# Two-layer decoder trunk: mixed operands of the output projection on VectorE, later block loads, one inverse root chain

## The chip, the cores and the metric

The kernel runs on one core of a Trainium2 chip. The metric is the device time of one execution in microseconds (us), the median of several. Below, PE is TensorE, DVE is VectorE, ACT is ScalarE, POOL is GpSimd, and SP is the sync engine, which here only issues DMAs. Each engine works through its own instructions in order, and an instruction that waits on a semaphore holds up everything behind it on its engine.

## The reference

Two residual layers on x of 1024 tokens by 1024 features, in float32. Cut to what matters:

```python
# layer 1: gated short convolution, width 2048
h = rms_norm(x, conv_norm)
b, c, u, z = split(h @ w_in, 4)          # w_in: 1024 x 8192
y = b * conv3(c * u) * silu(z)           # causal, depthwise, 3 taps
x1 = x + y @ w_out                       # w_out: 2048 x 1024
# layer 2: dilated attention, 3 groups of 16 heads of 64
h = rms_norm(x1, attn_norm)
qkv, z = h @ w_in2                       # q and k are RMS-normed per head
o = softmax-weighted merge of 3 dilated window attentions with a T5 bias
out = x1 + (o * silu(z)) @ w_out2
```

The RMS norm divides each token by a root mean square, so it is a factor per token, and the kernel applies it after the projection, as one over the root.

## The kernel before

**Matrix products.** Every float32 operand is split into a rounded part and a rest (a "block" is four 128x512 tiles with both parts), and a product of 128x512 outputs over 512 inputs is 12 matmuls (`product`, L303: L307 rounded by rounded, L309 rounded weight by rest, L310 the weight's rest). The split of a weight is `split_w`: a copy on ACT (L160), then a subtraction on DVE (L161).

**Seven products for eight.** Most of the projections go in pairs of weight columns through a Strassen scheme: seven products instead of eight. The loop `strassen` (L322) runs over pairs; within a pair the products come in the order 1, 2, 4 (of the pair before), 6, 5, 3 (of the pair before), 7. "Slot `at`" is the place of a product in that order, 0 to 6, and `between(n, at)` is called behind product `at` of pair n for the extra work that is spread over the pairs. `prepare` (L267) yields the weights of the next pair one slot at a time; four of its seven weights are sums and differences that POOL makes (tile `sr`, L281), each then split by L160 and L161. The moving operands are mixed likewise: blocks T[1] to T[4] are differences of the quarters of x (or y), B the plain ones.

Products 1, 6, 7 and 4 (4 runs in the next pair) accumulate in one PSUM tile `x`. ACT copies it out after product 1 (`m1`) and after product 6 (`u2`), both by L315; the product that comes next on that tile, 6 or 7, overwrites nothing before this copy has read it. So product 7 waits for the copy `u2`, and product 6 for the copy `m1`.

**The stages.** Layer 1's input projection is pairs 0 to 28 (NI = 29), each width block e of 128 channels taking two pairs, c and u with pr = 0, z and b with pr = 1. The results go through the gate (ACT's L371, POOL's L372, L584, L599), the taps (L378 to L380), DVE's L602 and L612, and `close` (L386), and are written to DRAM `ydc` (L387). The output projection of layer 1, by `out_pair` (L499), is pairs NI to NI+3 for one half of the width; its mixed operands are four differences of quarters of y, in DRAM `ymd`. The other half comes in plain products, `chunk` and `row` (L683, L688): `row(hf, dt)` loads the partial sum from DRAM `x1d` (L692), adds the product (L693), writes x1 back, and makes from it the operands of layer 2 (blocks e, f, d, the block `xb`, and tiles V1 and V3), and x1's square summed into `sqacc` on POOL (L721). Then come the pairs of layer 2's projection, numbered from 0 again.

**What the change touches.**
- `y_mix(i)` (L491), called at slot 0 of the four pairs with pr = 1 and e from 6 to 9: SP loads four tiles of `ydc` (L494), POOL subtracts four times (L496) and writes each difference to `ymd` (L497, issued by POOL).
- `moves` (L623): at which slot which block of the output projection is loaded by SP and split by ACT (L480) and DVE (L481).
- `stats` (L93): four matmuls of one column sum `sqacc` over partitions, L97 scales, and `rsqrt` (L59) runs a chain of ten small DVE steps (L63, then three times L65, L66, L67). Before, it runs for token half 0 at slot 3 of layer 2's pair 0 and for half 1 at slot 1 of pair 1. `spread` (L100) turns a column of the result into a row for all partitions by four PE transposes (L105); `rtok` goes to R1 (by ACT, L107), which the pairs with v and z use, and `ms2` through DVE (L111, L112) to a small tile for the norm of q and k.
- `third`, `fourth`, `lower` (L905 to L920): blocks T[3], T[4] and B[1, 1] of layer 2, made at the slots of the table `rest`. `fourth` and `lower` load x1 from DRAM (L677); `fourth` starts with the DVE step L914.

**What sets the order.** PE, and in places the other engines, run in program order. Elsewhere the Tile scheduler merges the engines' work by its own estimate, so the place of a DVE or POOL instruction can differ from the place in the code. Tiles named `f` come from a pool of 12 buffers, so a load into one waits for the release of the tile twelve before.

## Time and profile before

| | before |
|---|---|
| median of 3 runs | 1931.04 us (1928.29 to 1932.02) |
| the profiled execution, its own time | 1936.98 us |
| its span from first to last instruction | 1934.9 us |
| mean granted TensorE clock | 0.991 |
| busy PE | 1883.5 us (97%) |
| busy PE weight loads | 1541.6 us (80%) |
| busy DVE | 1518.0 us (78%) |
| busy ACT | 884.8 us (46%) |
| busy POOL | 978.2 us (51%) |
| HBM read and written | 194.62 MB and 76.03 MB |

All times of the trace are counted from the span's start. In a table of windows, each engine has its busy time and, in brackets, the number of instructions; PEclk is the clock that TensorE was granted, as a share of full speed. In a timeline, the first two columns are start and duration, and square brackets hold the time for which the engine stood idle ahead of the instruction and what ended it. In a list of waits, the columns are the total, the number of times and the longest.

The stages along the span: the start up to about 270 us, pairs with `y_mix` from 271 to about 420 us, the rest of layer 1's input projection to about 640 us, the output projection to about 818 us, layer 2's projection to about 1606 us, attention and the last projection from there to the end.

### The profile page before, as it was taken

How to read it: one execution, taken by the hardware profiler on the slowest of the kernel's cores; microseconds unless marked ns; L12 is line 12 of the kernel's file. 1: busy time of each engine (PE TensorE's matmuls, PEld its weight loads, DVE VectorE, ACT ScalarE, POOL GpSimd, SP SyncE). 2: the span in 40 equal slices, each digit the busy share in tenths (PEclk: the TensorE clock that was granted, in tenths of full speed). 3: DMA queues.
4: the chain of work that ended last, by engine and by line, in shares of the span. 5: the costliest groups of instructions: out<-in, count | busy, mean ns of one | idle time of the engine just before them, and what ended most of it. 6: DMA issues, size and time to landing. Idle time of an engine off the chain costs nothing. (4 is left out here: it accounts for less than half of the span.)

```text
span 1934.9 us, 30577 instructions
## 1 busy us (share of the span) xinstructions
PE 1883.5 (97%) x10814; PEld 1541.6 (80%) x10814; DVE 1518.0 (78%) x2789; ACT 884.8 (46%) x2039; POOL 978.2 (51%) x910
## 2 busy tenths in 40 slices
PE   8999999999999999989999999999999998989999
PEld 6888887778888788868888888888888886777877
DVE  7966778877665855678888788868888886988886
ACT  6533333333433534443344344434444437878880
POOL 1376677776666453525445544564454552433340
PEclk9999999999999999999999999999999999899999
DMA  6222234332323765323324332433232336897742
GB/s 220 78 80 89 88 104 151 126 129 90 92 73 92 264 226 207 131 82 109 110 87 136 104 112 85 136 104 112 85 131 88 131 126 242 258 298 229 228 143 88
DMA packets 121514, 264.29 MB, mean 137 GB/s; under 512 B 19134, under 2 KB 24478, under 8 KB 121360
## 3 DMA queue, kind: packets, MB, share of 16 engines
q1 hardware_dynamic: 94432, 178.99, 28.6%
q0 software_dynamic: 26928, 83.34, 12.9%
q8 instruction: 85, 1.39, 0.3%
q14 instruction: 69, 0.57, 0.1%
HBM read 194.62 MB, written 76.03 MB: 140 GB/s over the span
## 5 line engine op out<-in xcount | busy, mean ns | idle before, releaser
L161 DVE TENSOR_TENSOR ws<-sr,ws 128x512 fp32r<-128x512 f32 x288 | 270.0, 943 | 95.8 <-ACT ws L160 93.9
L160 ACT ACTIVATE ws<-sr 128x512 fp32r<-128x512 f32 x288 | 180.6, 630 | 353.8 <-PE pp L310 254.0
L281 POOL TENSOR_TENSOR sr<-wr 128x512 f32<-128x512 f32 x144 | 209.4, 1454 | 245.9 <-DMA wr<-in_conv_w_in 96.5
L161 DVE TENSOR_TENSOR ws<-wr,ws 128x512 fp32r<-128x512 f32 x248 | 267.5, 1080 | 78.6 <-ACT ws L160 78.0
L160 ACT ACTIVATE ws<-wr 128x512 fp32r<-128x512 f32 x248 | 155.7, 629 | 290.6 <-PE pp L310 243.5
L319 DVE TENSOR_TENSOR f<-pp,f 128x512 f32<-128x512 f32 x216 | 147.6, 683 | 70.2 <-PE pp L310 63.1
L1058 ACT ACTIVATE xs<-xs,nl 128x256 f32<-128x256 f32 (+2 forms) x384 | 160.8, 428 | 0.0
L315 ACT ACTIVATE f<-pp 128x512 f32<-128x512 f32 x240 | 139.4, 581 | 4.1 <-PE pp L310 4.0
L281 POOL TENSOR_TENSOR sr<-wr,sr 128x512 f32<-128x512 f32 x72 | 95.5, 1327 | 70.1 <-issue 59.1
L307 PE MATMUL pp<-blka,ws 128*128 128x512 f32 x328 | 127.8, 390 | 0.7 <-ACT f L315 0.7
L307 PE MATMUL pp<-blkb,ws 128*128 128x512 f32 x328 | 128.0, 390 | 0.0
L310 PE MATMUL pp<-blkb,ws 128*128 128x512 f32 x328 | 127.6, 389 | 0.0
L309 PE MATMUL pp<-blka,ws 128*128 128x512 f32 x328 | 127.6, 389 | 0.0
L310 PE MATMUL pp<-blka,ws 128*128 128x512 f32 x328 | 127.6, 389 | 0.0
L309 PE MATMUL pp<-blkb,ws 128*128 128x512 f32 x328 | 127.6, 389 | 0.0
L307 PE MATMUL pp<-blkg,ws 128*128 128x512 f32 x320 | 125.2, 391 | 2.1 <-ACT f L315 2.1
L310 PE MATMUL pp<-blkg,ws 128*128 128x512 f32 x320 | 125.2, 391 | 0.0
L309 PE MATMUL pp<-blkg,ws 128*128 128x512 f32 x320 | 125.2, 391 | 0.0
L307 PE MATMUL pp<-blke,ws 128*128 128x512 f32 x288 | 113.9, 396 | 10.0 <-ACT f L315 10.0
L1052 DVE CUSTOM_DVE_ANT_0 xs<-ps,bt 128x256 f32<-128x256 f32 (+2 forms) x384 | 102.7, 326 | 20.4 <-PE pt L1065 11.8
L307 PE MATMUL pp<-blkf,ws 128*128 128x512 f32 x296 | 117.6, 397 | 0.5 <-ACT f L315 0.5
L309 PE MATMUL pp<-blkd,ws 128*128 128x512 f32 x296 | 115.6, 391 | 0.0
(329 smaller groups left out, 5055.9 us busy)
## 6 DMA issues: line engine op xcount, KB each, us to landing
wr<-in_conv_w_in SPq DMA_DIRECT2D x128, 256.0 KB, 3.2
wr<-in_wqk SPq DMA_DIRECT2D x96, 256.0 KB, 3.2
qkd<-blkc POOLq DMA_DIRECT2D x48, 512.0 KB, 4.0
qk<-qkd SPq DMA_DIRECT2D x48, 512.0 KB, 5.1
f<-in_x SPq DMA_DIRECT2D x48, 256.0 KB, 4.5
f<-ydc SPq DMA_DIRECT2D x48, 256.0 KB, 5.6
wr<-in_wv SPq DMA_DIRECT2D x48, 256.0 KB, 3.1
vd<-blkc POOLq DMA_DIRECT2D x96, 128.0 KB, 2.8
```

Of the source, the lines that this page charges most:

```text
L160: nc.scalar.activation(t[:, 0], src, AF.Copy)
L161: nc.vector.tensor_tensor(t[:, 1], src, t[:, 0].bitcast(F32), op=OP.subtract)
L281: nc.gpsimd.tensor_tensor(t, x, y, op=op)
L307: nc.tensor.matmul(ps, w[:, 0, ws], b[:, k, 0], start=new and k == 0, stop=False, skip_group_check=skip)
L309: nc.tensor.matmul(ps, w[:, 0, ws], b[:, k, 1], start=False, stop=False, skip_group_check=skip)
L310: nc.tensor.matmul(ps, w[:, 1, ws], b[:, k, 0], start=False, stop=end and k == 3, skip_group_check=skip)
L315: nc.scalar.activation(t, ps, AF.Copy)
L319: nc.vector.tensor_tensor(m, ps, m, op=OP.add)
L1052: nc.vector.tensor_tensor_reduce(out=x, in0=flat[s][:, cols], in1=u["bt"][s][:, bs], op0=OP.add, op1=OP.min, scale=-1.0, scalar=3e38, accu ...
L1058: nc.scalar.activation(x, x, AF.Exp, bias=nm, scale=-1.0, accum_out=L)
```

## The change

1. `y_mix` is cut into single steps. Instead of four differences at once in each of four pairs, one difference is made in each of the pairs 9 to 24, called at slot 2: SP loads the one or two tiles that are still missing, DVE subtracts (L509 of the changed file), POOL issues the write (L510).
2. Four of the loads of mixed blocks in the output projection come later: T[2] into block g from slot 3 to slot 4 of pair NI, T[1] into c from slot 4 to 6, T[3] into e from slot 5 to 8 (pair NI has ten slots), T[4] into f from slot 7 of pair NI to slot 3 of pair NI+1.
3. `stats` handles all eight columns at once, at slot 4 of layer 2's pair 0, and the four spreads run at slots 2 to 5 of pair 1, `ms2` first, `rtok` second.
4. `fourth(0)` to `fourth(2)` and `lower(0)` to `lower(2)` move from the slots of layer 2's first two pairs into the loop over rows, behind `row(0, 7)` and ahead of `row(1, 3)` and `row(1, 7)`. `fourth(3)` and `lower(3)` stay in pair 0, at slots 5 and 6.

```diff
-    def stats(hf, pool, tmp):
-        h4 = slice(4 * hf, 4 * hf + 4)
+    def stats(pool, tmp):
         ps = pool.tile([P, HALF], F32, name="st", tag="st")
-        mean_square(tmp, sqacc, ps, 4, lambda t, j: t[:, hf * HALF + j * P:hf * HALF + (j + 1) * P])
-        nc.vector.tensor_scalar(ms2[:, h4], ps[:, :4], 1.0 / D, EPS, op0=OP.mult, op1=OP.add)
-        rsqrt(tmp, ms2[:, h4], 4, "rt", rtok[:, h4])
+        mean_square(tmp, sqacc, ps, 8, lambda t, j: t[:, j * P:(j + 1) * P])
+        nc.vector.tensor_scalar(ms2, ps[:, :8], 1.0 / D, EPS, op0=OP.mult, op1=OP.add)
+        rsqrt(tmp, ms2, 8, "rt", rtok)
...
-            def y_mix(i):
-                a11, a12, a22, a21 = (ftile() for _ in range(4))
-                for t, hf, e in ((a11, 0, i), (a12, 1, i), (a22, 1, i + 4), (a21, 0, i + 4)):
+            ym = {}
+
+            def y_mix(i, n):
+
+                def load(hf, e):
+                    t = ftile()
                     nc.sync.dma_start(t, ydc[hf, e])
-                for n, (t, x, y) in enumerate(((a12, a12, a11), (a22, a22, a12), (a11, a22, a11), (a21, a21, a22))):
-                    nc.gpsimd.tensor_tensor(t, x, y, op=OP.subtract)
-                    nc.gpsimd.dma_start(ymd[n + 1, i], t)
+                    return t
+
+                if n == 0:
+                    ym["a"], t = load(0, i), load(1, i)
+                    y = ym["a"]
+                elif n == 1:
+                    t, y = load(1, i + 4), ym.pop("v")
+                elif n == 2:
+                    t, y = ym.pop("a"), ym["v"]
+                else:
+                    t, y = load(0, i + 4), ym.pop("v")
+                x, y = (y, t) if n == 2 else (t, y)
+                nc.vector.tensor_tensor(t, x, y, op=OP.subtract)
+                nc.gpsimd.dma_start(ymd[n + 1, i], t)
+                if n < 2:
+                    ym["v"] = t
...
-                     (NI, 3): lambda: y_mixed(2, "g"), (NI, 4): lambda: y_mixed(1, "c"),
-                     (NI, 5): lambda: y_mixed(3, "e"), (NI, 7): lambda: y_mixed(4, "f"),
+                     (NI, 4): lambda: y_mixed(2, "g"), (NI, 6): lambda: y_mixed(1, "c"),
+                     (NI, 8): lambda: y_mixed(3, "e"), (NI + 1, 3): lambda: y_mixed(4, "f"),
...
-                if pr and not at and 6 <= e < 10:
-                    y_mix(e - 6)
+                if at == 2 and 0 <= n - 9 < 16:
+                    y_mix((n - 9) // 4, (n - 9) % 4)
...
+                    elif hf == 0:
+                        for j in range(3):
+                            fourth(j)
+                        for j in range(3):
+                            lower(j)
...
-                if (n, at) in ((0, 3), (1, 1)):
-                    stats(n, cst, sm)
-                elif (n, at) in ((0, 6), (1, 5)):
-                    spread(n, rtok, cst)
-                elif (n, at) in ((1, 0), (1, 6)):
-                    spread(at // 6, ms2, cst)
+                if (n, at) == (0, 4):
+                    stats(cst, sm)
+                elif n == 1 and 2 <= at < 6:
+                    spread(at % 2, ms2 if at < 4 else rtok, cst)
...
-            rest = {0: [(third, 0), (third, 1)], 1: [(third, 2)], 2: [(third, 3)], 3: [(fourth, 0), (fourth, 1)],
-                    4: [(fourth, 2)], 5: [(fourth, 3), (lower, 0)], 6: [(lower, 1), (lower, 2)], 7: [(lower, 3)]}
+            rest = {0: [(third, 0), (third, 1)], 1: [(third, 2)], 2: [(third, 3)], 5: [(fourth, 3)], 6: [(lower, 3)]}
```

The functions `third`, `fourth` and `lower` themselves are only moved up. In the changed file, lines from 93 up to `y_mix` stand one earlier than before, those behind it fifteen later up to the row loop, and `fourth`'s step L914 is L747.

How the instructions stand on three engines, before and after, without any time in it. POOL first, in a pair of layer 1 with `y_mix` before: `sr` are weight sums, L496 the differences of y and L497 their writes, L584 and L372 the gate.

```order
L281 TENSOR_TENSOR sr<-wr 128x512
L281 TENSOR_TENSOR sr<-sr,wr 128x512
L281 TENSOR_TENSOR sr<-wr 128x512
L496 TENSOR_TENSOR f<-f 128x512
L584 TENSOR_TENSOR f<-f,R 128x512
L497 DMA ymd<-f 128x512
L496 TENSOR_TENSOR f<-f 128x512
L372 TENSOR_TENSOR f<-f,R 128x512
L497 DMA ymd<-f 128x512
L496 TENSOR_TENSOR f<-f 128x512 x2
L281 TENSOR_TENSOR sr<-wr,sr 128x512
```

The same stretch of POOL in the changed kernel, in the second pair that makes a difference (pair 10):

```order
L280 TENSOR_TENSOR sr<-wr 128x512
L280 TENSOR_TENSOR sr<-sr,wr 128x512
L280 TENSOR_TENSOR sr<-wr 128x512
L510 DMA ymd<-f 128x512
L599 TENSOR_TENSOR f<-f,R 128x512
L510 DMA ymd<-f 128x512
L371 TENSOR_TENSOR f<-f,R 128x512
L280 TENSOR_TENSOR sr<-wr,sr 128x512
```

Four subtractions have left POOL between the third and the last `sr`; writes of the differences stand there in their place, each behind a subtraction on DVE.

SP next, in pair NI and behind it: the loads of mixed blocks (`ymd`), of x, and of the weights of the next output pairs (`conv_w_out`). Before:

```order
L479 DMA f<-ymd 128x512 x4
L505 DMA f<-in_x 128x512
L479 DMA f<-ymd 128x512 x8
L505 DMA f<-in_x 128x512 x2
L479 DMA f<-ymd 128x512 x2
L155 DMA wr<-in_conv_w_out 128x512 x2
L479 DMA f<-ymd 128x512 x2
L155 DMA wr<-in_conv_w_out 128x512 x2
L505 DMA f<-in_x 128x512 x2
```

After:

```order
L478 DMA f<-ymd 128x512 x4
L520 DMA f<-in_x 128x512
L478 DMA f<-ymd 128x512 x4
L520 DMA f<-in_x 128x512
L478 DMA f<-ymd 128x512 x3
L154 DMA wr<-in_conv_w_out 128x512
L478 DMA f<-ymd 128x512
L154 DMA wr<-in_conv_w_out 128x512 x3
L520 DMA f<-in_x 128x512 x2
L478 DMA f<-ymd 128x512 x4
```

Ahead of the first weight load stand eleven loads of mixed blocks instead of fourteen, ahead of the third twelve instead of sixteen, and the last four come behind the weights.

DVE last, from `row(1, 7)` into layer 2's pair 0. L693 is the row's addition, L670 the rest of a block's part, L712 and L715 make the tiles V1 and V3, L319 is the addition behind product 2, L779 the sum of squares for the norm of q and k. Before:

```order
L161 TENSOR_TENSOR ws<-sr,ws 128x512
L670 TENSOR_TENSOR blkg<-f,blkg 128x512 x3
L693 TENSOR_TENSOR f<-pp,f 128x512
L670 TENSOR_TENSOR blkd<-f,blkd 128x512
L161 TENSOR_TENSOR ws<-wr,ws 128x512
L712 SCALAR_TENSOR_TENSOR f<-f,attn_norm 128x512
L715 SCALAR_TENSOR_TENSOR f<-f,ng_73 128x512
L161 TENSOR_TENSOR ws<-wr,ws 128x512
L670 TENSOR_TENSOR xb<-f,xb 128x512
L670 TENSOR_TENSOR blkg<-f,blkg 128x512
L319 TENSOR_TENSOR f<-pp,f 128x512
L161 TENSOR_TENSOR ws<-sr,ws 128x512
```

After, from the same addition (now L708), where L318 is the addition behind product 2, L727 and L730 make V1 and V3, and L816 is the sum of squares:

```order
L708 TENSOR_TENSOR f<-pp,f 128x512
L160 TENSOR_TENSOR ws<-wr,ws 128x512
L685 TENSOR_TENSOR blkd<-f,blkd 128x512
L318 TENSOR_TENSOR f<-pp,f 128x512
L727 SCALAR_TENSOR_TENSOR f<-f,attn_norm 128x512
L160 TENSOR_TENSOR ws<-sr,ws 128x512
L730 SCALAR_TENSOR_TENSOR f<-f,ng_73 128x512
L816 TENSOR_REDUCE st<-f 128x16
L685 TENSOR_TENSOR xb<-f,xb 128x512
L685 TENSOR_TENSOR blkg<-f,blkg 128x512
```

The additions behind product 2 and the sum of squares have moved ahead of the last part of `xb`. Of the nine DVE steps of `fourth` and `lower` that are now called in the row loop, eight stand further up, ahead of the addition of `row(1, 3)`, and one right behind it.

More of the change, by code (lines that the diff above doesn't have):

```diff
@@ L721, in row, with third, fourth, lower @@
                     nc.gpsimd.tensor_tensor(sqacc[:, cs], sqacc[:, cs], sq, op=OP.add)
+            def third(i):
+                if i == 0:
+                    T[3] = block("g")
+                parts_of(T[3], i, V3[i])
+            def fourth(i):
+                if i == 0:
+                    T[4] = block("a")
+                t, kt = x1_tile(0, i + 4), i + 4
+                nc.vector.scalar_tensor_tensor(t, t, g2[:, kt:kt + 1], V1[i], op0=OP.mult, op1=OP.subtract)
+                parts_of(T[4], i, t)
+            def lower(i):
+                if i == 0:
+                    B[1, 1] = block("b")
+                parts_of(B[1, 1], i, x1_tile(1, i + 4), g2[:, i + 4:i + 5])
             chunk(0, 0, 0)
@@ L895, in between @@
                         f(i)
-                if (n, at) in ((0, 3), (1, 1)):
-                    stats(n, cst, sm)
-                elif (n, at) in ((0, 6), (1, 5)):
-                    spread(n, rtok, cst)
-                elif (n, at) in ((1, 0), (1, 6)):
-                    spread(at // 6, ms2, cst)
+                if (n, at) == (0, 4):
+                    stats(cst, sm)
+                elif n == 1 and 2 <= at < 6:
+                    spread(at % 2, ms2 if at < 4 else rtok, cst)
                 for f in due.pop((n, at), ()):
                     f()
-            def third(i):
-                if i == 0:
-                    T[3] = block("g")
-                parts_of(T[3], i, V3[i])
-            def fourth(i):
-                if i == 0:
-                    T[4] = block("a")
-                t, kt = x1_tile(0, i + 4), i + 4
-                nc.vector.scalar_tensor_tensor(t, t, g2[:, kt:kt + 1], V1[i], op0=OP.mult, op1=OP.subtract)
-                parts_of(T[4], i, t)
-            def lower(i):
-                if i == 0:
-                    B[1, 1] = block("b")
-                parts_of(B[1, 1], i, x1_tile(1, i + 4), g2[:, i + 4:i + 5])
-            rest = {0: [(third, 0), (third, 1)], 1: [(third, 2)], 2: [(third, 3)], 3: [(fourth, 0), (fourth, 1)],
-                    4: [(fourth, 2)], 5: [(fourth, 3), (lower, 0)], 6: [(lower, 1), (lower, 2)], 7: [(lower, 3)]}
+            rest = {0: [(third, 0), (third, 1)], 1: [(third, 2)], 2: [(third, 3)], 5: [(fourth, 3)], 6: [(lower, 3)]}
             last = strassen([sources(p) for p in pairs], pair, between, lambda: None)
```

## The prediction

> **What bounds the kernel now.** I read the page's busy times first, then PE's list of waits, then windows over the stages that the change touches, then the timelines of the engines at those waits.
>
> ```profile
> PE 1883.5 (97%) x10814; PEld 1541.6 (80%) x10814; DVE 1518.0 (78%) x2789; ACT 884.8 (46%) x2039; POOL 978.2 (51%) x910
> ```
>
> PE is busy for 97% of the span, so only two things can be won here: time in which PE stands still, and time in which it runs at a lower clock. Windows show both: the stage with y_mix, one pair inside it, one quiet pair after it, and the surroundings of the two longest waits.
>
> ```profile
> 270.00:456.00 186.00, 176.00 (x768) 143.14 (x767) 149.97 (x129) 63.83 (x111) 145.32 (x122) 1.00 0.38 129
> ...
> 396.00:417.00 21.00, 19.32 (x85) 15.69 (x84) 17.75 (x12) 6.77 (x12) 18.15 (x17) 1.00 0.35 124
> 459.00:480.00 21.00, 21.00 (x95) 17.38 (x94) 13.63 (x14) 7.32 (x13) 15.43 (x13) 1.00 0.23 77
> ...
> 676.00:682.00 6.00, 5.11 (x15) 4.07 (x16) 4.36 (x8) 1.36 (x3) 3.29 (x4) 0.72 0.68 246
> 838.00:846.00 8.00, 5.54 (x17) 4.51 (x18) 4.01 (x10) 2.59 (x4) 2.55 (x2) 0.57 0.47 164
> ```
>
> PE loses 10.0 us in 270 to 456, none in the quiet pair, and around 677 and 840 it also has a granted clock of 0.72 and 0.57. Its waits in 295 to 456, and the two in the window 800 to 885:
>
> ```profile
> PE pp L307 <- ACT f L315: 10.0, 8, 1.7
> ...
> PE st L105 <- DVE rtok L67: 6.1, 1, 6.1
> PE pp L309 <- DVE xb L670: 0.8, 1, 0.8
> ```
>
> The eight waits, 10.0 us, are product 7 waiting for the copy u2. Why this copy is late, POOL's timeline shows in one y_mix pair, and ACT's behind it:
>
> ```profile
> 320.00 1.74 POOL L496 TENSOR_TENSOR f<-f 128x512 f32<-128x512 f32 x1
> 321.71 1.72 POOL L584 TENSOR_TENSOR f<-f,R 128x512 f32<-128x512 f32 x1
> 323.38 0.57 POOL L497 DMA_DIRECT2D ymd<-f  x1
> ...
> 323.46 0.63 ACT L371 ACTIVATE f<-f 128x512 f32<-128x512 f32 x1 [4.46 <-POOL f L584]
> 324.00 0.58 ACT L315 ACTIVATE f<-pp 128x512 f32<-128x512 f32 x1
> ```
>
> ACT stands 4.46 us in front of the gate L371, whose input L584 stands on POOL behind a y difference; the copy u2 is the next instruction on ACT, so it is late by as much. The last weight sum stands behind the remaining differences too, and the next weight loads behind its release of the raw weights, which would explain the waits one pair on.
>
> **Part 1, y_mix.** It takes 4 x 1.3 us off POOL in four pairs (16 instructions in all), and leaves the writes, 0.57 us each, spread one to a pair.
>
> ```profile
> L496 POOL TENSOR_TENSOR f<-f x16: 1281/1306/1737, 279.0 to 411.9; 128x512 f32<-128x512 f32 x16
> ```
>
> In return each of 16 pairs gets one subtraction on DVE. The trace has none of this shape from y, so the nearest rows bound it: the product of two SBUF tiles (L612) at 0.69, and a weight's subtraction (L161) at 1.77 while POOL works.
>
> ```profile
> 490.97 0.69 DVE L612 TENSOR_TENSOR vb<-f 128x512 f32<-128x512 f32 x1 [1.53 <-POOL f L611]
> ...
> 479.67 1.77 DVE L161 TENSOR_TENSOR ws<-wr,ws 128x512 fp32r<-128x512 f32 x1
> ```
>
> I take 1.3 us, in the middle, since POOL is busy for three quarters of a pair. That is 21 us of DVE in all, and the quiet pair leaves 7 of 21 us free, so by itself it costs PE nothing; if DVE had no room, it would cost up to 1.77 per pair. [...]
>
> What counts more is what waits behind it. The loads now stand just ahead of the subtraction on SP, right behind the weight loads, and DVE waits for the landing.
>
> ```profile
> DMA to landing us min/median/max: 4.0/5.1/5.6
> ...
> 469.95 4.26 SPq L155 DMA_DIRECT2D wr<-in_conv_w_in  x3
> ...
> 476.35 0.69 DVE L319 TENSOR_TENSOR f<-pp,f 128x512 f32<-128x512 f32 x1 [1.26 <-PE pp L310]
> ...
> 482.55 1.74 POOL L584 TENSOR_TENSOR f<-f,R 128x512 f32<-128x512 f32 x1
> ...
> 485.38 0.58 ACT L315 ACTIVATE f<-pp 128x512 f32<-128x512 f32 x1
> ...
> 486.96 0.39 PE L307 MATMUL pp<-blke,ws 128*128 128x512 f32 x1
> ```
>
> On the clock of the quiet pair (which has the gate): the last weight load is issued by 474.2, so the y load lands at 478.2 to 479.8 by the y loads of before (first line), and DVE has subtracted by 481.6 at the latest. L319, behind it on DVE, slips from 476.4 to about 480.5. POOL is at its weight sums until 482.55, then comes the write (0.57), then L584, which needs L319. The copy u2 ended at 485.96, 1.0 us ahead of product 7 at 486.96; the write leaves 0.4 us of that. In the pairs without the gate no such chain stands ahead of u2. So I leave 0 to 4 us (0 to 1 in each of the four or so tightest pairs) of the 10.0 and take 1.5: **gain 8.5**, from 6 to 10.
>
> **Part 2, later block loads.** At 676.89 product 6 of pair NI+1 waits for the copy m1:
>
> ```profile
> 676.89 0.50 PE L307 MATMUL pp<-blkg,ws 128*128 128x512 f32 x1 [2.06 <-ACT f L315]
> ...
> 674.37 0.63 ACT L480 ACTIVATE blkf<-f 128x512 fp32r<-128x512 f32 x1 [2.71 <-DMA f<-ymd]
> ...
> 675.75 0.61 ACT L160 ACTIVATE ws<-wr 128x512 fp32r<-128x512 f32 x1
> 676.27 0.58 ACT L315 ACTIVATE f<-pp 128x512 f32<-128x512 f32 x1
> ...
> 669.41 1.13 SPq L479 DMA_DIRECT2D f<-ymd  x2
> 674.37 0.81 SPq L155 DMA_DIRECT2D wr<-in_conv_w_out  x2
> ...
> 679.71 1.27 POOL L281 TENSOR_TENSOR sr<-wr 128x512 f32<-128x512 f32 x1 [0.32 <-DMA wr<-in_conv_w_out]
> ```
>
> ACT stood 2.71 us in front of the last pieces of block f, which SP issued only from 669.41. These now come behind the weights, in slot 3 of pair NI+1, so m1 can be copied right behind product 1, at about 672 (PE was ready for product 6 at 676.89 - 2.06 = 674.8), and the wait of 2.06 goes. With it goes the slow stretch behind it: (1 - 0.72) x 6 = 1.7 us. Next in line is the sum for weight 6 (POOL started its first at 679.71, waiting for the load that SP issued at 674.37), with product 7 some 5 us behind product 6; ahead of that load on SP now stand four block loads fewer, so it comes some 4 us earlier and product 7 finds it. The blocks themselves are needed a pair later. **Gain 3.5**, from 2 to 3.8. [...]
>
> **Parts 3 and 4, the start of layer 2.** The wait of 6.1 is the spread of rtok. Its chain of ten small steps began here, and ended ten microseconds later:
>
> ```profile
> 829.88 0.17 DVE L63 TENSOR_SCALAR rtok<-ms 128x4 int32<-128x4 int32 x1
> ...
> 830.77 0.75 DVE L914 SCALAR_TENSOR_TENSOR f<-f,attn_norm 128x512 f32<-128x512 f32 x1
> ...
> 840.15 0.16 DVE L67 SCALAR_TENSOR_TENSOR rtok<-rtt,rtok 128x4 f32<-128x4 f32 x1
> ```
>
> Most of it is work of fourth and lower between the steps. With those moved away and the spreads a pair later, the chain stands on DVE without a break (some 2 us at 0.17 to 0.2 each; the four columns more cost nothing that these rows show), and its first reader comes about five products, 13 us, later. So 6.1 goes, and 2.0 us more of the slow clock behind it (product 1 took 841.20 to 845.90, 4.7 us, against 2.7 for 12 of the matmuls of which the quiet pair had 95 in 21.00 us).
>
> ```profile
> 840.46 1.08 PE L105 MATMUL st<-ident,rtok 128*128 128x128 f32 x4 [6.11 <-DVE rtok L67]
> 841.20 0.78 PE L307 MATMUL pp<-blke,ws 128*128 128x512 f32 x1
> ...
> 845.90 0.60 PE L105 MATMUL st<-ident,ms 128*128 128x128 f32 x4
> ```
>
> But the moved work has to go somewhere. Its six loads now stand on SP between the row loads, and wait for free f tiles; six ACT splits and nine DVE steps go ahead of or among rows (1,3) and (1,7), which end in xb, and product 6 already waited for that by 0.8.
>
> ```profile
> 802.39 8.89 SPq L692 DMA_DIRECT2D f<-x1d  x3
> ...
> 812.96 0.69 DVE L693 TENSOR_TENSOR f<-pp,f 128x512 f32<-128x512 f32 x1 [1.42 <-PE pp L310]
> ...
> 819.88 0.68 DVE L693 TENSOR_TENSOR f<-pp,f 128x512 f32<-128x512 f32 x1
> ...
> 826.50 0.69 DVE L670 TENSOR_TENSOR xb<-f,xb 128x512 fp32r<-128x512 f32 x1
> ```
>
> The x1 load of row (1,3), issued in the first row's three before 803, now waits, by the order, for a tile that DVE frees at about 812; landing some 4 us later, as the y loads did, it lets DVE add at about 817 instead of 812.96, so row (1,7) comes at about 823 instead of 819.88. In the order, the addition behind product 2 and the sum of squares now stand ahead of the last xb. I put that at 829 to 831 instead of 827.2: product 6 waits 2 to 4 us more, and if the gap passes 2 us, 0 to 1.7 us of slow clock come with it. Of 8.1, I take 5.1 back: **gain 3**, from -1 to 6.
>
> **The sum.** 8.5 + 3.5 + 3 = 15 off 1936.98 (span 1934.9 and 2 us around it) gives 1922. The profiled execution lies 5.9 above the median 1931.04, so the forecast is **1916**. From the ends: 10 + 3.8 + 6 = 19.8 gives 1911, 6 + 2 - 1 = 7 gives 1924.
>
> **Rivals.**
> - *The rows become the bound.* The late row loads push xb further than 831, and all of the 8.1 comes back as wait for xb and slow clock. For it: SP works in order, and the moved loads wait for tiles. Against: fourth needs only what row (0,7) has read. Then 8.5 + 3.5 - 2 = 10: 1921.
> - *The y_mix stalls stay.* Some of the eight waits came a pair behind POOL's surplus, by late weight loads, and a write still stands ahead of L584. If the waits stay at 1 us in each such pair, part 1 gives 2 in place of 8.5: 15 - 6.5 = 8.5, 1922.5; with the rows late too, 1927.5. [...]
> - *Slower: the load under the subtraction.* The wait moves from POOL in four pairs to DVE in sixteen. It decides from a y load that lands later than about 481.2 (7 us after its issue): with 1.77 for the subtraction and 0.6 for L319, L584 starts after 483.1 + 0.4, and product 7 waits. A landing of 8.5 us would cost 1.5 in each of 16 pairs, 24 us; with 10 + 3.5 + 3 gained, 1931.04 + 7.5 = 1938.5. Against: the y loads of before took 5.6 at most, though four were issued at a time.
> - *No change.* The scheduler hides the stalls anew elsewhere: the first wait given back by DVE in y pairs, the last by xb: 1930.
>
> **How the numbers follow.** The forecast's own case has 0.53, rows 0.19, stalls that stay 0.13, slower 0.07, no change 0.08. A measurement of this kernel tells about 0.2%, 3.9 us, from no change, so faster means below 1927.2. The first two are faster, of the third 0.10 and 0.03 within; of the first two I put 0.02 within as well. Faster 0.80, same 0.13, slower 0.07. The range goes from 1909, just beyond the best ends, to 1928, which holds stalls and rows together; outside lie slower, no change and little else.
>
> **What would show it.** In the changed profile: PE's wait L307 on the copy L314 in 270 to 456 falls from 10.0 to below 4, while DVE shows idle time ended by the y load. POOL's busy time falls by about 21 us, DVE's rises by 11 to 28. At product 6 of pair NI+1 no gap and a clock of 1.00. The spread of rtok waits for nothing; the rows' wait shows as L309 on xb, 3 to 5 us. I am wrong if PE's waits on the copy stay at 8 or more, if ACT or DVE show a new chain at product 7 of pairs 9 to 24, or if xb costs over 8 us.

## The result, and the profile after

| | before | after |
|---|---|---|
| median of the runs shown with the result | 1932.02 us (5 runs, 1928.29 to 1935.58) | 1920.91 us (5 runs, 1917.34 to 1924.36) |
| ratio to before, 95% interval | | 0.9939 (0.9919 to 0.9960) |
| the profiled execution, its own time | 1936.98 us | 1917.34 us |
| its span | 1934.9 us | 1915.5 us |

The kernel became faster by 11.1 us, where 15 were forecast (1916, range 1909 to 1928). The spans of the two profiled executions differ by more, 19.4 us. To see where, I take the same product in both traces and subtract its start after from its start before; between two such points the growth of the difference is what that stage gained. The last point is the first score matmul of the attention, called "the mark" below: 1606.77 us before, 1594.25 after.

| stage, on the clock of before | forecast | after |
|---|---|---|
| 270 to 601, y_mix (part 1) | 8.5 | 10.3 |
| 601 to 700, pairs NI and NI+1 (part 2) | 3.5 | 2.2 |
| 700 to 813, rows | 0 | -0.2 |
| 813 to the mark, start of layer 2 (parts 3 and 4) | 3 | 0.5 |
| the mark to the end, attention (not changed) | 0 | 6.8 |

So 12.5 us stand ahead of the mark (with -0.3 from the start of the program), and the other 6.8 come in code whose instructions and order are the same in both kernels. That last stage took between 320 and 330 us in all fourteen traces of this study, whatever was changed; it is not a gain. What moves it is, in the main, the clock: in this stage PE stood at half clock for 13.9 us in the shortest (319.9 us, "part 1 alone" below; 0.995 in the mean of the whole run) and for 28.0 us in the longest (330.1, "without part 4"; 0.993). Before it was 24.7 us (a clock of 0.96 in this stage) and after 14.3 (0.98); half of that difference is 5.2 of the 6.8 us.

PE's waits in the window 250 to 900 of the changed kernel, in the columns of before:

```profile
PE pp L306 <- ACT f L314: 3.6, 4, 1.5
PE pp L308 <- DVE xb L685: 3.0, 1, 3.0
PE pp L306 <- ACT xb L684: 2.1, 1, 2.1
PE st L104 <- DVE f L110: 0.4, 1, 0.4
```

Of product 7's eight waits all but one are gone, and so is the 6.1 at the spread. What is left on the copy L314 is one wait of 1.27 in the y_mix stage, one of 0.16 later, one of 1.49 at product 7 of pair NI+1, and 0.66 in pair NI+3; and xb, which cost 0.8 before, now costs 5.1 in two pieces. The windows of the stages say the same; the last one is the start of layer 2, with a clock of 0.84:

```profile
270.00:456.00 186.00, 184.73 (x815) 152.64 (x814) 136.62 (x148) 67.13 (x116) 124.21 (x107) 1.00 0.36 115
640.00:700.00 60.00, 58.51 (x258) 48.12 (x257) 42.73 (x57) 28.58 (x51) 35.68 (x32) 1.00 0.68 234
808.00:830.00 22.00, 16.76 (x67) 13.00 (x66) 16.38 (x28) 7.56 (x13) 11.69 (x7) 0.84 0.14 49
```

The moved subtraction, by its line: the durations (minimum, median, maximum in ns), and what DVE stood waiting for ahead of it.

```profile
L509 DVE TENSOR_TENSOR f<-f x16: 692/1172/1523, 256.5 to 546.1; 128x512 f32<-128x512 f32 x16
...
  DMA f<-ydc: 37.7, 12
```

It takes 1.17 us (1.3 was assumed), and DVE does stand 37.7 us in front of its loads, 3 us at a time; this is cover that DVE had.

The start of layer 2, on DVE, POOL, ACT and PE in turn, from the additions of row (1,3) and row (1,7), both L708, to the last part of product 6, which starts at 811.90:

```profile
805.09 0.68 DVE L708 TENSOR_TENSOR f<-pp,f 128x512 f32<-128x512 f32 x1
...
809.97 0.68 DVE L708 TENSOR_TENSOR f<-pp,f 128x512 f32<-128x512 f32 x1
...
813.97 1.17 DVE L727 SCALAR_TENSOR_TENSOR f<-f,attn_norm 128x512 f32<-128x512 f32 x1
815.28 1.53 DVE L160 TENSOR_TENSOR ws<-sr,ws 128x512 fp32r<-128x512 f32 x1
816.73 1.88 DVE L730 SCALAR_TENSOR_TENSOR f<-f,ng 128x512 f32<-128x512 f32 x1
818.54 0.70 DVE L816 TRANSPOSE_TENSOR_REDUCE st<-f 128x16 f32<-128x512 f32 x1
819.16 0.65 DVE L685 TENSOR_TENSOR xb<-f,xb 128x512 fp32r<-128x512 f32 x1
...
806.86 4.34 POOL L280 TENSOR_TENSOR sr<-wr 128x512 f32<-128x512 f32 x1 [0.24 <-DMA wr<-in_wqk]
...
814.62 0.63 ACT L159 ACTIVATE ws<-sr 128x512 fp32r<-128x512 f32 x1 [2.76 <-POOL sr L280]
815.15 0.61 ACT L815 ACTIVATE f<-f 128x512 f32<-128x512 f32 x1
815.67 0.61 ACT L684 ACTIVATE xb<-f 128x512 fp32r<-128x512 f32 x1
...
816.34 0.49 PE L306 MATMUL pp<-xb,ws 128*128 128x512 f32 x1 [2.06 <-ACT xb L684]
819.86 0.79 PE L308 MATMUL pp<-xb,ws 128*128 128x512 f32 x1 [3.03 <-DVE xb L685]
```

The same two steps before, where product 6 starts at 823.59, V1 on DVE and the rounded part of xb on ACT:

```profile
823.29 1.90 DVE L712 SCALAR_TENSOR_TENSOR f<-f,attn_norm 128x512 f32<-128x512 f32 x1
...
825.22 0.63 ACT L669 ACTIVATE xb<-f 128x512 fp32r<-128x512 f32 x1 [2.98 <-DVE f L712]
```

Two things are late here, counted from the start of product 6. The rounded part of xb (ACT L684) starts 3.8 us behind it, and 1.6 before. It is made from V1 (DVE L727), which ends 1.6 us later than before, since row (1,7)'s addition stands 1.9 us ahead of product 6 where it stood 3.7. V1 is there at 815.14; only the 0.5 us from then to 815.67 is the weight split ahead on ACT, which had waited 2.76 us for POOL, whose weight sum had taken 4.34 us in place of 1.3 while DVE ran one step after the other. And the rest of xb (DVE L685) starts 7.3 us behind product 6's start, and 2.9 before: between V1 and it stand a weight split and V3 (L730), each longer than the 0.68 and 0.75 that they take elsewhere in this trace, and the sum of squares. The chain of ten small steps, on the other hand, is as forecast: from 828.34 to 830.33 without a break.

```profile
828.34 0.17 DVE L63 TENSOR_SCALAR rtok<-ms 128x8 int32<-128x8 int32 x1
...
830.16 0.17 DVE L67 SCALAR_TENSOR_TENSOR rtok<-rtt,rtok 128x8 f32<-128x8 f32 x1
```

### The profile page after: what moved, and what is told of

The parts are those of the page before. It is cut to its first block, busy times and chain, and to the rows that moved or that the text cites. A ratio compares the mean times of both kernels' runs of the same rounds, so it can differ in the third digit from the quotient of the medians.

```text
span 1915.5 us, 30556 instructions
## 1 busy us (share of the span) xinstructions
PE 1877.1 (98%) x10814; PEld 1538.3 (80%) x10814; DVE 1490.9 (78%) x2794; ACT 883.5 (46%) x2039; POOL 957.8 (50%) x894
## 5 line engine op out<-in xcount | busy, mean ns | idle before, releaser
L160 DVE TENSOR_TENSOR ws<-sr,ws 128x512 fp32r<-128x512 f32 x288 | 260.3, 910 | 83.6 <-ACT ws L159 81.6
L160 DVE TENSOR_TENSOR ws<-wr,ws 128x512 fp32r<-128x512 f32 x248 | 256.4, 1035 | 75.1 <-ACT ws L159 74.6
L318 DVE TENSOR_TENSOR f<-pp,f 128x512 f32<-128x512 f32 x216 | 147.6, 683 | 62.6 <-PE pp L309 54.7
L314 ACT ACTIVATE f<-pp 128x512 f32<-128x512 f32 x240 | 139.5, 581 | 9.3 <-PE pp L309 9.3
L308 PE MATMUL pp<-blkd,ws 128*128 128x512 f32 x296 | 116.6, 394 | 0.0
L306 PE MATMUL pp<-blkd,ws 128*128 128x512 f32 x296 | 116.4, 393 | 0.0
```

The lines of the kernel that those rows point to most:

```text
L160: nc.vector.tensor_tensor(t[:, 1], src, t[:, 0].bitcast(F32), op=OP.subtract)
L306: nc.tensor.matmul(ps, w[:, 0, ws], b[:, k, 0], start=new and k == 0, stop=False, skip_group_check=skip)
L308: nc.tensor.matmul(ps, w[:, 0, ws], b[:, k, 1], start=False, stop=False, skip_group_check=skip)
L314: nc.scalar.activation(t, ps, AF.Copy)
L318: nc.vector.tensor_tensor(m, ps, m, op=OP.add)
```

## The experiments

The theory after the result: part 1 works as forecast; part 2 only uncovers the next wait; and in layer 2 the gain of part 3 is eaten by part 4, the moved steps. Rivals: the parts need each other, or the single chain itself makes xb late. All stage gains below are against the one trace of before, in us: y_mix (270 to 601), NI (601 to 700), L2 (813 to the mark).

| kernel | y_mix | NI | L2 | mark at | waits at xb |
|---|---|---|---|---|---|
| after | 10.3 | 2.2 | 0.5 | 1594.3 | 2.1 + 3.0 |
| after, again | 10.7 | 3.7 | 1.9 | 1590.5 | 2.1 + 3.0 |
| part 1 alone | 11.8 | 0.4 | 0.4 | 1594.8 | 0.8 |
| part 2 alone | 0.8 | 2.3 | -0.2 | 1603.1 | 1.0 |
| parts 3 and 4 alone | 0.9 | -0.3 | 1.2 | 1605.9 | 2.1 + 3.0 |
| without part 4 | 10.3 | 2.5 | 5.8 | 1589.8 | 1.0 |
| the same, spreads further apart | 9.8 | 3.5 | 8.1 | 1586.1 | 0.8 |
| differences spread, on POOL | 1.8 | 0.7 | -0.4 | 1604.9 | 0.8 |
| differences on DVE, four at once | 3.0 | 0.9 | 0.2 | 1602.5 | 0.8 |
| only block f later | 10.9 | -0.4 | 8.2 | 1587.5 | 0.8 |
| block e later still | 12.3 | 1.9 | 8.5 | 1583.8 | 1.0 |
| lower moved | 11.0 | 2.7 | 4.2 | 1588.2 | 2.9 + 0.8 |
| fourth moved | 9.1 | 3.8 | 4.8 | 1588.7 | 2.0 + 0.8 |

How far such a figure repeats is seen where the code is the same: the y_mix stage gained 9.1 to 12.3 in the nine traces with part 1, and 0.8 and 0.9 in the two with nothing changed there. The two other columns repeat better: NI gave 2.2 to 3.8 with part 2 as in the change, L2 0.5 to 1.9 with all of parts 3 and 4 and 8.1 to 8.5 without part 4 and with the spreads apart. So a difference of 3 us in the y_mix column, or of 2 in the others, is not read as anything in one trace.

**The changed kernel again.** No edit.

> The changed kernel once more, to see how far its mark and its waits repeat. Expected: mark (start of the first score matmul) 1594.3 within 1.5 us, waits at xb near 5 us again with a stretch at half clock behind them, product 7's waits between 250 and 620 between 1 and 2 us in all, one wait of 0.2 to 1.5 at product 7 of pair NI+1.

Measured: 1918.90 us against 1935.53 before on the same chip, ratio 0.9915 (0.9896 to 0.9934). The waits at xb are the same to 0.02 us, product 7's waits in the y_mix stage 0.5, none at product 7 of pair NI+1; both are below what I had expected. The mark was 1590.5, 3.8 earlier, so it does not repeat within the 1.5 that I had expected: 1.5 of it is the wait at product 7 that was not there this time, and the stretch at half clock behind xb was 3.4 us long and not 6.8.

**Each part alone.** `y_mix` as in the change, nothing else:

```diff
-                if pr and not at and 6 <= e < 10:
-                    y_mix(e - 6)
+                if at == 2 and 0 <= n - 9 < 16:
+                    y_mix((n - 9) // 4, (n - 9) % 4)
```

> The kernel before with part 1 alone (y_mix as 16 single steps on VectorE). If the parts are independent: product 7's waits in 270 to 456 fall from 10.0 to below 2, the waits of 2.06 at product 6 and of 6.1 at the spread stay, and the mark (start of the first score matmul) goes from 1606.8 to about 1596.5. If the gain needs the later block loads as well, the mark stays above 1600.

Measured (one run): 1916.53 us, mark 1594.8; product 7's waits in the stage fell to one of 0.19. Part 1 is independent of the others, and it alone brings the mark to where the whole change had it in its first trace.

The four loads later, nothing else:

```diff
-                     (NI, 3): lambda: y_mixed(2, "g"), (NI, 4): lambda: y_mixed(1, "c"),
-                     (NI, 5): lambda: y_mixed(3, "e"), (NI, 7): lambda: y_mixed(4, "f"),
+                     (NI, 4): lambda: y_mixed(2, "g"), (NI, 6): lambda: y_mixed(1, "c"),
+                     (NI, 8): lambda: y_mixed(3, "e"), (NI + 1, 3): lambda: y_mixed(4, "f"),
```

> The kernel before with part 2 alone (four block loads later). Theory A (ScalarE no longer waits for the last block, and the next to come is product 7 waiting for u2 behind weight 6's split, since the second raw weight's load waits for a split on VectorE behind the block e): no wait at product 6, one of about 1.5 at product 7, no slow clock there, mark at about 1604.6, that is 2.1 earlier. Theory B (as forecast: the load comes 4 us earlier and nothing is left): mark at about 1603.0 and no wait at product 7.

Measured: 1933.78 us, mark 1603.1. No wait at product 6, 1.41 at product 7, no slow clock there (NI gained 2.3): the waits are theory A's. The mark would fit B better, but 0.8 of its 3.6 arose in the y_mix stage, where nothing was changed, so it says little.

Parts 3 and 4, nothing else: the `stats`, `spread` and `rest` of the change, with fourth and lower in the row loop.

> The kernel before with parts 3 and 4 alone (one chain, spreads in pair 1, fourth and lower in the row loop). Theory A: the spread's wait of 6.1 goes, xb's waits rise to about 5 with a stretch at half clock, mark within 1 us of 1606.8. As forecast: xb's wait 3 to 5, mark about 1603.8.

Measured: 1930.32 us, mark 1605.9, xb 2.06 + 3.02 with a slow stretch of 6.8 us. Theory A. The single chain and the moved steps together gain 1.2 us in their stage, which is not told from nothing.

**Part 4 undone.**

```diff
-                    elif hf == 0:
-                        for j in range(3):
-                            fourth(j)
-                        for j in range(3):
-                            lower(j)
...
-            rest = {0: [(third, 0), (third, 1)], 1: [(third, 2)], 2: [(third, 3)], 5: [(fourth, 3)], 6: [(lower, 3)]}
+            rest = {0: [(third, 0), (third, 1)], 1: [(third, 2)], 2: [(third, 3)], 3: [(fourth, 0), (fourth, 1)],
+                    4: [(fourth, 2)], 5: [(fourth, 3), (lower, 0)], 6: [(lower, 1), (lower, 2)], 7: [(lower, 3)]}
```

> The changed kernel with its fourth part undone: fourth(0..2) and lower(0..2) back at the slots of layer 2's first two pairs; stats still once, the spreads still in pair 1. The mark is the start of the attention's first score matmul, 1594.25 us in the changed kernel and 1606.77 before. Theory A (the steps moved into the row loop are what makes xb late, and the wait that left the spread has come back there): product 6's two waits of 2.07 and 3.03 fall to one of about 0.8, no slow clock between 800 and 850, mark at about 1587 (1585 to 1589), time about 1914. Theory B (xb is late because of the single stats or of the scheduler's order, not of the moved steps): the waits stay near 5 us, mark 1593 to 1595, time about 1921. Theory C (fourth and lower are too late without the 6.1 us that the old wait gave them): xb is on time but a new wait of 2 to 6 us stands at product 4 or 3 of pair 0, mark 1590 to 1595.

Measured: 1920.28 us (6 runs; 1914 was expected by theory A), ratio 0.9921 (0.9903 to 0.9940). PE's waits in the same window, 250 to 900:

```profile
PE st L104 <- DVE f L110: 2.9, 1, 2.9
PE pp L306 <- ACT f L314: 2.9, 4, 1.2
PE pp L308 <- DVE xb L685: 1.0, 1, 1.0
```

Theory A for xb: 1.0 in place of 5.1 and no slow clock (L2 gained 5.8), so the moved steps made it late, and not the chain. The mark, 1589.8, is behind theory A's 1585 to 1589, for another wait. That is theory C in a form of its own: not a product but the second spread waits, 2.9 us, for the one PSUM tile that DVE had to read first (L110), since DVE was at the pieces of block b. DVE's timeline there:

```profile
835.06 1.81 DVE L688 SCALAR_TENSOR_TENSOR blkb<-f,attn_norm,blkb 128x512 fp32r<-128x512 f32 x2
836.79 0.68 DVE L160 TENSOR_TENSOR ws<-wr,ws 128x512 fp32r<-128x512 f32 x1
837.39 0.70 DVE L110 STREAM_TRANSPOSE f<-st 128x512 f32<-128x512 f32 x1
```

**Spreads further apart.** On top of the last edit:

```diff
-                elif n == 1 and 2 <= at < 6:
-                    spread(at % 2, ms2 if at < 4 else rtok, cst)
+                elif n == 1 and at in (2, 4, 5, 6):
+                    spread(at // 4 if at < 5 else at - 5, ms2 if at < 5 else rtok, cst)
```

> As no_move, with the spreads at slots 2, 4, 5, 6 of pair 1 in place of 2, 3, 4, 5. In no_move the second spread of ms2 stood 2.88 us for the PSUM tile that VectorE had not yet read (L110), since VectorE was at the late pieces of block b. Theory A (the second spread only came too soon behind the first): no wait over 0.5 us between 820 and 870, mark at about 1587 (1586 to 1588). Theory B (VectorE is full there and the wait moves to the next product or spread): a wait of 1.5 to 3 us remains, mark 1589 to 1590.

Measured: 1916.37 us (6 runs), ratio 0.9916 (0.9902 to 0.9929); mark 1586.1. No wait at a spread is left in the window:

```profile
PE pp L306 <- ACT f L314: 3.4, 4, 1.5
PE pp L308 <- DVE xb L685: 0.8, 1, 0.8
```

Theory A, with all of the 8.1 us that the start of layer 2 had to give. In the whole time it isn't told apart from the changed kernel (0.9939 and 0.9915 in its two measurements): it is 4 to 8 us better at the mark, and the last stage scatters by 10.

**Engine or spreading.** The difference on POOL, one in each pair:

```diff
-                nc.vector.tensor_tensor(t, x, y, op=OP.subtract)
+                nc.gpsimd.tensor_tensor(t, x, y, op=OP.subtract)
```

> As p1_only, with the subtraction on GpSimd (one in each of 16 pairs) in place of VectorE. Theory A (what cures is that the work is spread; GpSimd has room for one difference of 1.3 us and a write of 0.57 per pair): product 7's waits between 270 and 620 are below 3 us, stage time as p1_only within 2 us. Theory B (what cures is the change of engine, since GpSimd's work stands ahead of the gate): each of the pairs with a gate still waits 1 us or so, 5 to 12 us in all.

Measured: 1930.50 us, stage gain 1.8 with seven waits of 0.4 to 2.4, 8.5 us in all, one in every second pair. The timeline of POOL, then of ACT, at the longest:

```profile
434.99 1.74 POOL L510 TENSOR_TENSOR f<-f 128x512 f32<-128x512 f32 x1
436.68 1.28 POOL L281 TENSOR_TENSOR sr<-sr,wr 128x512 f32<-128x512 f32 x1
437.92 1.29 POOL L281 TENSOR_TENSOR sr<-wr 128x512 f32<-128x512 f32 x1
439.17 1.28 POOL L600 TENSOR_TENSOR f<-f,R 128x512 f32<-128x512 f32 x1
...
440.48 0.63 ACT L371 ACTIVATE f<-f 128x512 f32<-128x512 f32 x1 [7.39 <-POOL f L600]
```

Theory B: a single difference ahead of the weight sums and the gate's product is enough to make ACT wait for the gate, with u2 behind it.

The four at once, as before, on DVE:

```diff
-                    nc.gpsimd.tensor_tensor(t, x, y, op=OP.subtract)
+                    nc.vector.tensor_tensor(t, x, y, op=OP.subtract)
```

> The kernel before with the four differences of y_mix on VectorE, still four at once in four pairs. Theory A (spreading cures): four subtractions of 0.7 to 1.8 us in a row put VectorE's splits and additions back by 3 to 7 us, and waits of 5 us or more remain in 270 to 456. Theory B (the engine cures): the waits fall below 2 us as in p1_only.

Measured: 1934.31 us, stage gain 3.0: two waits of 2.77 and 2.05, each with a slow stretch behind it (the clock of the whole run was 0.989, and 0.991 before). DVE's timeline at the first (the three other differences are the row of x3), then ACT's:

```profile
317.74 1.71 DVE L496 TENSOR_TENSOR f<-f 128x512 f32<-128x512 f32 x1 [4.32 <-DMA f<-ydc]
...
321.07 2.01 DVE L496 TENSOR_TENSOR f<-f 128x512 f32<-128x512 f32 x3
323.00 0.69 DVE L602 TENSOR_TENSOR vb<-pp,f 128x512 f32<-128x512 f32 x1
...
323.72 0.72 ACT L378 ACTIVATE g<-vb,conv_w 128x512 f32<-128x512 f32 x1 [2.45 <-DVE vb L602]
```

By the sum of the waits in 270 to 456, 5.1 us, it is theory A, but the wait has moved, much as the rival "the load under the subtraction" had it: ACT waits for DVE's L602 behind the differences, and u2 stands behind that. It needs four of them at once. Neither the engine nor the spreading alone gives more than 3 of the 10 us; the two do it together.

**Block f alone.** As the spreads further apart, with g, c and e at their old slots.

```diff
-                     (NI, 4): lambda: y_mixed(2, "g"), (NI, 6): lambda: y_mixed(1, "c"),
-                     (NI, 8): lambda: y_mixed(3, "e"), (NI + 1, 3): lambda: y_mixed(4, "f"),
+                     (NI, 3): lambda: y_mixed(2, "g"), (NI, 4): lambda: y_mixed(1, "c"),
+                     (NI, 5): lambda: y_mixed(3, "e"), (NI + 1, 3): lambda: y_mixed(4, "f"),
```

> As nm_spread, with only block f loaded later; g, c and e again at slots 3, 4 and 5 of pair NI. Theory A (product 6's wait was block f alone; product 7's wait of 1.2 to 1.5 comes from a raw weight's load that waits for a split on VectorE behind block e, and with e loaded earlier this split comes earlier): no wait at product 6 and below 0.8 at product 7 of pair NI+1. Theory B (all four moves are needed, or product 7's wait doesn't depend on block e): a wait of 1.2 us or more at product 7 or some at product 6 remains.

Measured: 1913.12 us (one run). No wait at product 6, so block f was its cause; but 2.52 at product 7, with a slow stretch (NI -0.4, and 2.2 to 3.8 with part 2 as in the change): theory A falls where it said that e loaded earlier would make the split earlier. Block e's four parts still stand ahead of the split on DVE.

**Block e later still.** As the spreads further apart, with e at slot 1 of pair NI+1:

```diff
-                     (NI, 8): lambda: y_mixed(3, "e"), (NI + 1, 3): lambda: y_mixed(4, "f"),
+                     (NI + 1, 1): lambda: y_mixed(3, "e"), (NI + 1, 3): lambda: y_mixed(4, "f"),
```

> As nm_spread, with block e loaded at slot 1 of pair NI+1 in place of slot 8 of pair NI. Theory A (product 7's wait in pair NI+1 comes from the second raw weight's load, which waits for a split on VectorE behind block parts): with e's four parts behind the split, that load is issued 3 us or more ahead of product 6 (2.0 in nm_spread, 0.35 in f_only), and product 7 doesn't wait for u2. Theory B (block e itself is then too late for product 7): product 7 waits 1 to 4 us for block e.

Measured: 1913.50 us (one run), mark 1583.8, the earliest of all. The load is issued 3.9 us ahead of product 6, as theory A says, and product 7 waits 0.27 for u2; of theory B 0.75 came true, for block e. Over the traces, product 7's wait follows the landing of the second half of that raw weight, in us behind the start of product 6:

| | f only | after | part 2 alone | without part 4 | lower moved | spreads apart | after, again | fourth moved | e later |
|---|---|---|---|---|---|---|---|---|---|
| landing | 4.16 | 3.10 | 3.03 | 2.85 | 2.61 | 1.82 | 1.60 | 1.45 | 0.83 |
| product 7's wait for u2 | 2.52 | 1.49 | 1.41 | 1.24 | 0.99 | 0.21 | 0.00 | 0 | 0.27 |

Each is the landing less 1.6, until block e itself is in the way. The load waits, by the order of the program, until DVE has split the last piece of the raw weight that held its buffer before (L160), and this split stands among the block parts: in all fourteen traces the first half of the load is issued 0.02 us behind the end of that split. The two traces of the changed kernel differ less by the issue (1.83 and 2.04 us ahead of product 6) than by the landing of the second half, which took 4.5 and 3.3 us.

**Half of the moved steps.** As the spreads further apart, with lower(0..2), or fourth(0..2), in the row loop:

```diff
+                    elif hf == 0:
+                        for j in range(3):
+                            lower(j)
```

```diff
+                    elif hf == 0:
+                        for j in range(3):
+                            fourth(j)
```

> As nm_spread, with only lower(0..2) moved into the row loop (three loads, three VectorE steps, three ScalarE steps ahead of rows (1,3) and (1,7)). Theory A (it is the sum of nine moved VectorE steps that makes the rows late, so that product 2's addition and the sum of squares come ahead of xb): three steps fit in VectorE's idle time, xb's wait stays 0.8 to 1.2, mark 1586 to 1587. Theory B (it is the x1 load of row (1,3), queued on the sync engine behind moved loads that wait for tiles): xb's wait is 2 us or more already.

> As nm_spread, with only fourth(0..2) moved into the row loop (three loads, six VectorE steps, three ScalarE steps). Theory A: xb's wait 0.8 to 2, mark 1586 to 1588, clearly less than the 5 us of all nine steps. Theory B: 2 us or more, as with lower alone.

Measured: 1915.43 and 1914.26 us (one run each); xb 2.9 + 0.8 and 2.0 + 0.8, each with a slow stretch (L2 4.2 and 4.8, and 8.1 without a move). That is theory B's number, but only in small part its cause. The x1 load of row (1,3) landed 9.4 and 9.9 us ahead of product 6, in place of 16.4 without a move, and the addition behind it came 1.4 and 1.6 us later. But row (1,7)'s addition, from which xb is made, came 2.2 and 4.2 us ahead of product 6, and 3.7 without a move: with fourth moved it isn't late at all, and xb is. What made xb late is to be seen in DVE's and POOL's timelines, of "lower moved" first:

```profile
808.26 4.67 DVE L685 TENSOR_TENSOR blkd<-f,blkd 128x512 fp32r<-128x512 f32 x1
812.96 0.75 DVE L727 SCALAR_TENSOR_TENSOR f<-f,attn_norm 128x512 f32<-128x512 f32 x1
...
808.61 1.30 POOL L280 TENSOR_TENSOR sr<-sr,wr 128x512 f32<-128x512 f32 x1
809.87 1.28 POOL L280 TENSOR_TENSOR sr<-wr 128x512 f32<-128x512 f32 x1
811.11 1.25 POOL L736 TENSOR_TENSOR sqacc<-sqacc,f 128x512 f32<-128x512 f32 x1
```

and of "fourth moved":

```profile
809.63 4.26 DVE L727 SCALAR_TENSOR_TENSOR f<-f,attn_norm 128x512 f32<-128x512 f32 x1
...
809.56 1.31 POOL L280 TENSOR_TENSOR sr<-sr,wr 128x512 f32<-128x512 f32 x1
810.81 1.30 POOL L280 TENSOR_TENSOR sr<-wr 128x512 f32<-128x512 f32 x1
812.06 1.27 POOL L736 TENSOR_TENSOR sqacc<-sqacc,f 128x512 f32<-128x512 f32 x1
```

One DVE step of 0.7 us takes 4.67 us in the one and 4.26 in the other: it ends 0.6 us behind the end of POOL's third step in a row. The moved steps shift DVE against POOL so that the step ahead of xb meets this run of three. Theory A falls, and B explains 1.5 us in one of the two. In the changed kernel it is the other way round: there POOL's weight sum took 4.34 us, from 806.86 to 811.20, while DVE ran seven steps of 0.7 us from 806.36 to 810.65 without a break, the last of them row (1,7)'s addition at 809.97. What in the two engines makes such a step long is not shown: these are durations and places, and no run tried it by itself.

## Why the prediction was right, point by point

**What bounds the kernel.** Right. PE's waits and its clock account for what was gained ahead of the mark, and the idle time of DVE (37.7 us in front of the y loads) cost next to nothing.

**Part 1: 8.5 forecast, 10.3 and 10.7 measured, 11.8 alone.** The mechanism was right: POOL late, gate late, u2 late. The residue of 1.5 was right as well (1.43 and 0.50). The gain is larger than the waits that went, 10.0 - 1.4 = 8.6, for two reasons that were not in the sum: each of the eight waits also had a slow first matmul behind it (0.33 to 0.34 us to the next one, as from 324.63 to 324.97, in place of 0.23), and the stage moves from one trace to another (0.8 and 0.9 with nothing changed in it, 9.1 to 12.3 with part 1). One by-product was wrong: DVE's busy time was to rise by 11 to 28 us, and it fell, from 1518.0 to 1490.9. In 270 to 620 the splits of sums got shorter, which the groups show, before and after:

```profile
L161 DVE TENSOR_TENSOR ws<-sr,ws 128x512 fp32r<-128x512 f32 x71 | 93.8, 1330 | 39.0 <-ACT ws L160 38.8
```

```profile
L160 DVE TENSOR_TENSOR ws<-sr,ws 128x512 fp32r<-128x512 f32 x73 | 84.3, 1167 | 22.3 <-ACT ws L159 21.9
```

That POOL's lighter load is the reason is not shown. With the differences spread but still on POOL, POOL is as busy as before (974.5 us against 978.2), and yet DVE's busy time is 1486.2 and these splits take 1143 ns. How the steps of the two engines fall on each other may be the reason; that was not tried by itself. In the quiet pair of before, a split of a raw weight took 0.68 us at 476.96, when POOL stood idle, and another 1.77 at 479.67, when POOL was at its weight sums of 479.60 and 480.84.

**Part 2: 3.5 forecast, 2.2 and 3.7 measured.** The wait at product 6 and the slow stretch went, as forecast. The step that failed is "it comes some 4 us earlier and product 7 finds it": against product 6 the raw weight's load was issued 1.8 us ahead, and 2.5 before. Of these 2.5, 2.06 was product 6's own wait, so against the moment at which PE was ready the load came 1.3 us earlier (1.8 for 0.5) and not 4. Not the queue of block loads held it, but the buffer, which DVE's split frees late. Whether product 7 then waits is open from run to run, 0 to 1.5 us.

**Parts 3 and 4: 3 forecast, 0.5 and 1.9 measured.** The removal was right to the number (8.1, as "spreads further apart" shows). Of what comes back, 5.1 was forecast and 7.6 and 6.2 came: 4.3 us of waits at xb in both traces, where 2 to 4 were forecast, a slow stretch of 6.8 us in one and 3.4 in the other, which at a clock of 0.50 costs about half its length (at most 1.7 was allowed for), and 0.2 to 0.4 at a spread. The place was forecast, and the lateness of the rows in kind: row (1,3)'s addition 4.0 us forecast and 3.8 measured (it stands 6.8 us ahead of product 6 and stood 10.6 ahead), row (1,7)'s 3.1 forecast and 1.8 measured. The sum of squares ahead of the last part of xb was forecast too. What was missing is the length of DVE's steps there: the split and V3 ahead of that part took 1.53 and 1.88 us, 2.0 more than their 0.68 and 0.75, while POOL ran a weight sum (814.54, 1.72) and a sum of x1's squares (816.78, 1.27). That the clock drops once a gap passes 2 us was my estimate from the one gap of 2.06, and no run shows such a limit: at the gaps of 2.06 and 3.03 at xb it fell to 0.50, while "without part 4" has a gap of 2.88 at the spread and lost no more than that by it. And the sign, a wait of 3 to 5 us on the rest of xb, came in two pieces, 3.0 there and 2.1 on the rounded part, for which none was forecast. On the clock of before, xb was done at 831.5 (829 to 831 forecast). The rival "the rows become the bound", 1921, is what the first measurement looks like, 1920.9; in the second the sum at the mark is 16.3 and nearer to the forecast. That rival's sum takes 2 us more than the whole 8.1 back; with 8.1 it would be 1919. Between the two this can't be settled by the total, since the last stage alone moves it by 10 us.

**The total.** That it came within 4 us of the forecast has some luck in it. In the first trace part 1 lay 1.8 above its forecast, and part 2 and layer 2 lay 1.3 and 2.5 below; and the last stage by itself moves the total by more than any of these.

**The other rivals.** The stalls did not stay. The load under the subtraction did not come to pass in the change (the y loads landed in time in all but one or two pairs), but it did with four at once. That moves within the program only move the stalls was true of part 4, and in some traces of about half of part 2 (2.06 at product 6 went, up to 1.5 at product 7 came).

## What to carry to other kernels

Where a step is moved out of a stage in which PE waits, look at what PE waits for in the stage that receives it: here the single chain and later spreads had already taken the cost away, and the move of fourth and lower on top gave back 6 to 8 us. A buffer's release, and not the place in the load queue, can be what times a load: ask who reads the old contents last. And check a small gain against the stage that was changed, at a mark in the trace, when a later stage scatters by more than the gain.

## What the runs showed of the hardware

**When the clock dropped.** In the traces of before and after, the clock in each slow stretch is 0.50, and the stretches are 3.41, 6.83 or 10.24 us long (but for a last one that the end of the trace cuts). Between 60 and 1560 us there are two before and one after. Before, the one from 677.94 (3.41 us) comes behind PE's gap of 2.06 us, which ended at 676.89, and cost half its length, 1.7 us, besides; the one from 838.37 (6.83 us) starts within the gap of 6.11 that ended at 840.46. After, the one from 819.19 (6.83 us) starts within the second of xb's two gaps, 2.06 and 3.03 us with 0.5 between them. Behind PE's other waits in that range, of up to 1.68 us before and 1.49 after, there is none.

The length of one gap alone does not tell the cases apart. Before, a gap of 0.83 us at xb was followed by the eight one-column matmuls of the statistics (0.95 us in all), and the matmuls behind them stood 0.23 us apart; with the differences spread on POOL the same gap of 0.83 and the same eight matmuls were followed by matmuls 0.43 apart from 827.24 on, and in "part 2 alone" a gap of 0.98 and the eight by matmuls 0.43 apart from 824.95 to 828.36. And "without part 4" has a gap of 2.88 us at the spread, yet its L2 gain is only 2.3 below that with the spreads further apart, which has no such gap; with half clock for 3.41 us on top it would be 4.6. What decides is not shown by these runs.

**Long steps on DVE and POOL.** A DVE step of 0.7 us took 1.77 (before, 479.67) beside weight sums on POOL, and 4.67 and 4.26 ("lower moved" at 808.26, "fourth moved" at 809.63) beside three POOL steps in a row; a POOL step of 1.3 us took 4.34 (after, 806.86) beside seven DVE steps in a row. The cause was not tried by itself.
